# Nine channel blocks by seven products instead of eight, and the seam from up to down

## The chip, the cores and the metric

The kernel runs on one core of a Trainium2 chip. Its time is the device time of one execution in microseconds (us). The core has five engines that run side by side, each through its own list of instructions in order: TensorE (PE, matrix products, with its weight loads as PEld), VectorE (DVE), ScalarE (ACT), GpSimd (POOL) and SyncE (SP, which here issues most of the DMA transfers). An instruction waits until the semaphores that it names have been raised by what it depends on, and everything behind it on its engine waits with it.

## The reference

One layer of a hybrid encoder trunk on 512 tokens of width 1024, in float32. Four token mixers and a gated merge come first, then cross-attention, then the gated MLP that this text is about:

```python
hf = _rms_norm(x, norm_ffn_pre[l])
u = _dwconv_causal(hf @ w_up[l], ffn_dw[l]) + ffn_dw_b[l]
u_g, u_v = jnp.split(u, 2, axis=-1)
yff = (jax.nn.silu(u_g) * u_v) @ w_down[l]
x = x + _rms_norm(yff, norm_ffn_post[l])
```

`w_up` is 1024 x 5632 (2816 gate channels and 2816 value channels), `w_down` 2816 x 1024. The convolution runs along the tokens, has three taps and a weight per channel.

## The kernel before, in words

**Precision.** Each factor of a product is split into a high and a low half (`split_weights`, `split_to`: ACT rounds the high half, called `wh`, `hth`, `tokh`, with a CAST; DVE subtracts for the low half, `wl`, `htl`, `tokl`). `mm3` (line 245 through `matmul`) then makes three matmuls: high by high, high by low, low by high. Split weights lie in four buffers each for high and low, used in turn (`weights_tile`), so a tile can be split when PE has left the tile four before it.

**Up.** The 2816 channels are 22 blocks (NF) of 128, numbered j. A *plain* block (`plain(j, i)`; i is 0 for gate, 1 for value) is 8 x 3 matmuls of 512 tokens into one PSUM bank, so a channel block is 48 of them. A *seven* (`seven(j)`) forms gate and value of one j together: seven half-size products by a Strassen-like scheme, 7 x 4 x 3 = 84 matmuls of 256 tokens. POOL forms three sums of weights for it (lines 1755 to 1759), its weights are split in four tiles (loads a, b, c, d), and five pieces of work follow, `body_a` to `body_d` and `end`, called a to e here. c and e both use the tile that c splits (`z.w`). The seven's two results lie in one bank of `sc` (`z.r1`) and one of `tr` (`z.r2`); pieces are joined by ACT copies (`mu`) and DVE adds (lines 1786, 1797, 1801).

After the matmuls `done` puts the bias and the last tap on with ACT and adds the other two taps with DVE (line 627, called taps here); `product_of` then makes silu(gate) * value into `qa`, one tile of four parts for each pair of channel blocks (11 pairs, q = 0 to 10).

The jobs of up run interleaved: a(j), plain(j-1, 0), b, first half of plain(j-1, 1), c, d, second half, e, for j = 5, 7, ... 19. The blocks 20 and 21 follow as four plain blocks.

**Down.** It multiplies the 11 pairs, again by seven products per pair: M1, M6 (job 0) and M5, M7 (job 1) in a first phase, M2, M3 and M4 in a second. (q, job) names a weight tile of the first phase. Each M has two banks, one for each token tile t. The tiles come by SP (`load_parts`, line 594) into four buffers `dw` in turn, two of which are the `wq` buffers of the sevens; ACT and DVE split them (lines 1673 and 1674), and split the activations of pair q too (`activations`). For this, sums of a pair's four parts are needed (`down_sums`, lines 1684 to 1686, three DVE instructions of 256 columns), into places made free by `down_places`. Line 1920 is a POOL difference for the second phase.

**Order.** `run_blocks` fetches (loads and splits) about four jobs ahead of the one whose matmuls it writes. The order on each engine that results is then made by a scheduler when the program is built.

Of the kernel before, what the change touches and what calls it, by code (L numbers as in the profile page):

```python
# [25 lines left out]
P = 128  # L26
S = 512
# [59 lines left out]
def hybrid_layer(ctx: ExitStack, tc: tile.TileContext, a: dict, out: bass.AP):  # L87
# [520 lines left out]
    def seven_banks(phase):  # L608
        names = (("M2", "sc"), ("M3", "tr"), ("M4", "mm")) if phase else (("M1", "sc"), ("M6", "tr"), ("M5", "mm"),
                                                                         ("M7", "av"))  # L610
        return {name: [bank(tag) for _ in range(2)] for name, tag in names}
# [1027 lines left out]
    def open_ffn():  # L1639
        bg.drain("n1")  # L1640
        close(ns.work_)
        close(ns.xp_)
        close(ns.xm_)
        ns.fp_, ns.fp = new_pool("ffn", False)
        ns.work = ns.fp
        ns.quart = [ns.fp.tile([P, 4, S // 2], F32, tag=f"qa{q}", name="qa") for q in range(NF // 2)]
        ns.tok = [ns.fp.tile([P, 4, 4, S // 2], F32R, tag=n, name=n) for n in ("tokh", "tokl")]
        ns.post = ns.fp.tile([P, D], F32, name="g_ffn")
        ns.dw = {"dw": 1}
        G.dma_start(ns.post, a["norm_ffn_post"][0].partition_broadcast(P))  # L1650
# [25 lines left out]
    def down_places(tag, n):  # L1676
        x = ns.fp.tile([P, 2 * n, S // 2], F32, tag=tag, name="pairs")
        ns.pair_sums += [x[:, 2 * i:2 * i + 2] for i in range(n)]

# [8 lines left out]
    def up_jobs():  # L1688
# [126 lines left out]
        def early_places():  # L1815
            ns.pair_sums = []
            down_places(f"qa{NF // 2 - 1}", 2)

# [7 lines left out]
        pairs = {j: seven(j) for j in range(5, NF - 2, 2)}  # L1826
# [6 lines left out]
        for q, j in enumerate(pairs, EARLY - 1):  # L1833
# [25 lines left out]
            if j == NF - 3:  # L1859
                yield then(lambda: down_places("z7", 2))  # L1860
            yield d
            yield then(lambda j=j, f=second_half: f(j - 1))
            if j == NF - 3:
                yield then(sums_of(2))
# [3 lines left out]
        def late_places():  # L1868
            down_places("tokh", NF // 2 - 4)
            ns.quart[-1] = ns.fp.tile([P, 4, S // 2], F32, tag="tokl", name="qa")  # L1870

        yield then(late_places)
        yield plain(NF - 2, 0, sums_of(3))
        yield plain(NF - 2, 1, sums_of(4))
        yield plain(NF - 1, 0, sums_of(5))
        yield plain(NF - 1, 1)

    def down_jobs():
# [16 lines left out]
        def activations(phase, q):  # L1895
# [16 lines left out]
            else:  # L1912
# [3 lines left out]
                if 6 <= q + 2 < pairs:  # L1916
# [91 lines left out]
        def ends():  # L2008
# [5 lines left out]
            def whole(name, t, x, pieces=1):  # L2014


                for c in range(pieces):
                    cut = slice(c * S // pieces, (c + 1) * S // pieces)
                    ps = bank("av") if c else None
# [30 lines left out]
        def body(phase, q, job, ws):  # L2050
            if (q, job) == (0, 0):
                banks.update(seven_banks(phase))
# [61 lines left out]
```

## Time and profile before

| what | us |
|---|---|
| median of 3 runs (1032.75 to 1033.51) | 1033.33 |
| the profiled execution's own time | 1035.12 |
| its span, first to last instruction | 1033.3 |
| PE / DVE / ACT / POOL busy | 1024.4 / 864.0 / 534.4 / 263.5 |
| granted PE clock, mean over the span | 0.999 |

The profile is one execution. Its page gives the busy time of each engine, a chain of work followed back from the last instruction, and groups of instructions by source line. The trace behind it can be asked for the waits of an engine, for the busy time of each engine in given stretches, and for single instructions in order of time: start, length, engine, line, operation, output<-inputs, partitions x elements, count, and in brackets how long the engine had been idle before and what released it. A matmul's end is modelled; the distance from one start to the next is what a matmul costs in a dense stretch.

### The profile page before, as it was taken

The page shows a single profiled execution, that of the slowest core. Times are in us where ns is not written, and L with a number is a line of the kernel's source. Part 1 is how long each engine was busy: PE and PEld are TensorE (multiplying, and loading weights), DVE is VectorE, ACT ScalarE, POOL GpSimd, SP SyncE. Part 2 cuts the span into 40 slices and gives each one's busy share as a digit, 9 for nine tenths or more (in the row PEclk, how much of TensorE's full clock was granted, in tenths as well). Part 3 has the DMA queues.
Part 4 walks back from the last instruction along what each step waited for, and adds up shares of the span by engine and source line. Part 5 has one row for each costly group of instructions (what it writes and reads, how often), then busy time and mean ns, then how long its engine had stood idle before and what let it go on. Part 6 is the DMA issues. An engine that isn't in the chain of part 4 may idle for free.

```text
span 1033.3 us, 15189 instructions
## 1 busy us (share of the span) xinstructions
PE 1024.4 (99%) x5477; PEld 883.0 (85%) x5477; DVE 864.0 (84%) x1323; ACT 534.4 (52%) x893; POOL 263.5 (26%) x270
## 2 busy tenths in 40 slices
PE   9999999999999999999999999999999999999997
PEld 8888888888888988888888899999899899888886
DVE  7899999796878667888687898787989897799886
ACT  5322222376565466766543665655455455466662
POOL 4001000100011214442100031039177557226202
PEclk9999999999999999999999999999999999999999
DMA  7954344844434255767448834233456576626852
GB/s 248 317 176 106 104 147 143 280 143 115 141 102 140 63 157 137 195 184 188 154 146 264 262 123 123 82 97 116 134 164 209 180 225 210 197 81 187 274 161 82
DMA packets 194128, 169.40 MB, mean 164 GB/s; under 512 B 25295, under 2 KB 165692, under 8 KB 194053
## 3 DMA queue, kind: packets, MB, share of 16 engines
q1 hardware_dynamic: 187315, 145.08, 46.9%
q10 hardware_dynamic: 4178, 14.82, 3.9%
q0 software_dynamic: 2560, 8.54, 2.7%
q8 instruction: 43, 0.70, 0.3%
q14 instruction: 32, 0.26, 0.1%
HBM read 142.18 MB, written 26.23 MB: 163 GB/s over the span
## 4 chain that ended last, share of the span: by engine, by line
PE 95%; DVE 2%; DMA 1%; ACT 1%; issue 1%; POOL 0%; POOLq 0%; DVEq 0%; SPq 0%; ACTq 0%
PE ps_mm L245 41%; PE ps_av L245 26%; PE ps_tr L245 15%; PE ps_sc L245 11%; PE ps_tr L251 1%; PE ps_mm L463 1%; PE ps_av L463 1%; DVE e L860 0%; DMA xs<-in_x 0%; DMA ptl<-turned 0%; DVE e L1133 0%; DVE ptl L879 0%; ACT wh L202 0%; ACT e L1139 0%; DVE qk L820 0%
## 5 line engine op out<-in xcount | busy, mean ns | idle before, releaser
L202 ACT CAST wh<-wr 128x1024 fp32r<-128x1024 f32 (+1 forms) x124 | 129.5, 1046 | 188.6 <-PE ps_mm L245 70.4
L203 DVE TENSOR_TENSOR wl<-wr,wh 128x1024 fp32r<-128x1024 f32 (+1 forms) x124 | 165.3, 1334 | 30.0 <-ACT wh L202 29.5
L245 PE MATMUL ps_mm<-hth,wh 128*128 128x512 f32 (+1 forms) x472 | 173.5, 376 | 0.1
L245 PE MATMUL ps_mm<-htl,wh 128*128 128x512 f32 (+1 forms) x472 | 173.5, 376 | 0.0
L245 PE MATMUL ps_mm<-hth,wl 128*128 128x512 f32 (+1 forms) x472 | 173.2, 375 | 0.0
L245 PEld LDWEIGHTS ps_mm<-hth,wh 128*128 128x128 f32 x472 | 87.1, 188 | 15.7 <-ACT hth L164 0.3
L245 PEld LDWEIGHTS ps_mm<-hth,wl 128*128 128x128 f32 x472 | 87.0, 188 | 15.7
L245 PEld LDWEIGHTS ps_mm<-htl,wh 128*128 128x128 f32 x472 | 87.0, 188 | 15.2
L245 PE MATMUL ps_av<-htl,wh 128*128 128x512 f32 (+1 forms) x264 | 97.8, 370 | 0.0
L245 PE MATMUL ps_av<-hth,wh 128*128 128x512 f32 (+1 forms) x264 | 97.7, 370 | 0.0
L245 PE MATMUL ps_av<-hth,wl 128*128 128x512 f32 (+1 forms) x264 | 97.6, 370 | 0.0
L700 DVE SCALAR_TENSOR_TENSOR y<-y,par,y 128x508 f32<-128x508 f32 (+29 forms) x120 | 83.0, 733 | 0.0
L245 PEld LDWEIGHTS ps_av<-htl,wh 128*128 128x128 f32 x264 | 49.6, 188 | 8.1
L245 PEld LDWEIGHTS ps_av<-hth,wl 128*128 128x128 f32 x264 | 49.7, 188 | 8.0
L245 PEld LDWEIGHTS ps_av<-hth,wh 128*128 128x128 f32 x264 | 49.6, 188 | 8.0
L1673 ACT CAST wh<-dw 128x1024 fp32r<-128x1024 f32 x32 | 33.7, 1052 | 21.6 <-PE ps_av L245 8.1
L1674 DVE TENSOR_TENSOR wl<-dw,wh 128x1024 fp32r<-128x1024 f32 x32 | 39.6, 1243 | 5.5 <-ACT wh L1673 5.5
L245 PE MATMUL ps_tr<-htl,wh 128*128 128x512 f32 (+1 forms) x112 | 40.6, 363 | 0.0
L245 PE MATMUL ps_tr<-hth,wh 128*128 128x512 f32 (+1 forms) x112 | 40.6, 362 | 0.0
L245 PE MATMUL ps_tr<-hth,wl 128*128 128x512 f32 (+1 forms) x112 | 40.5, 361 | 0.0
L1920 POOL TENSOR_TENSOR qa<-qa 128x256 f32<-128x256 f32 x11 | 26.6, 2425 | 49.2 <-DVE wr L1674 25.2
L1127 POOL TENSOR_SCALAR fbias<-ck,cq 128x128 f32<-128x128 f32 (+3 forms) x32 | 21.3, 671 | 67.9 <-DVE st L1133 62.4
(558 smaller groups left out, 2739.1 us busy)
## 6 DMA issues: line engine op xcount, KB each, us to landing
wr<-in_w_in SPq DMA_DIRECT2D x38, 512.0 KB
wr<-in_w_gate SPq DMA_DIRECT2D x32, 512.0 KB
wr<-in_w_up SPq DMA_DIRECT2D x28, 512.0 KB
dw<-sums SPq DMA_DIRECT2D x44, 256.0 KB
wr<-in_w_branch SPq DMA_DIRECT2D x16, 512.0 KB
wq<-in_w_up SPq DMA_DIRECT2D x16, 512.0 KB
wp<-in_w_down ACTq DMA_DIRECT2D x14, 512.0 KB
sums<-wp ACTq DMA_DIRECT2D x14, 512.0 KB
```

The lines of the kernel that those rows point to most:

```text
L202: last_weights[:] = [order(A.copy(hi, raw[:, :n])).ins, low.tensor_tensor(lo, raw[:, :n], hi.bitcast(F32), ALU.subtract).ins]
L203: low.tensor_tensor(lo, raw[:, :n], hi.bitcast(F32), ALU.subtract).ins]
L245: steps_of[:] = [PE.matmul(ps, lhs, rhs, start=start, stop=stop, skip_group_check=again).ins]
L251: turns.append(PE.transpose(ps, x, ident[:n, :n]).ins)
L463: keep(PE.matmul(banks[c][:, :S // 2], w[p == 1][:, k, c * P:(c + 1) * P], ht[p == 2][:, i * 4 + k, :S // 2], start=(i, p, k) == (0, 0, 0) ...
L700: ins = V.scalar_tensor_tensor(dst[:, s:], src[:, :S - s], pc("conv_dw", k * 4 + j), dst[:, s:], ALU.mult, ALU.add)
L1127: G.tensor_scalar(bias[:, :w], ck[j][:, :w], -1.0, cq[:, qt, head:head + 1], ALU.mult, ALU.add)
L1673: A.copy(hi, x)
L1674: return V.tensor_tensor(lo, x, hi.bitcast(F32), ALU.subtract).ins
L1920: G.tensor_tensor(z[:, 1], z[:, 2], z[:, 1], ALU.subtract)
```

## The change

Block 21 becomes a ninth seven, interleaved with the plain block 20 as the others are. It then needs its working tiles (`tokh`, `tokl`, `z7`, the `wq` buffers) to the very end of up. So the places move: the last pair's activations get a tile of their own (`qlast`) where the gain `g_ffn` lay, the gain is loaded into `tokl` when up is over, and the sums of pair 3 are made after the last product of up, those of pairs 4 and 5 during down. Since the last seven holds a bank of `sc` and one of `tr`, M1, M6, M5, M7 are put in `mm`, `av`, `sc`, `tr` instead of `sc`, `tr`, `mm`, `av`, and the second phase likewise.

```diff
-    def seven_banks(phase):
-        names = (("M2", "sc"), ("M3", "tr"), ("M4", "mm")) if phase else (("M1", "sc"), ("M6", "tr"), ("M5", "mm"),
-                                                                         ("M7", "av"))
-        return {name: [bank(tag) for _ in range(2)] for name, tag in names}
+    def seven_banks(phase, tags=("sc", "tr", "mm", "av")):
+        names = ("M2", "M3", "M4") if phase else ("M1", "M6", "M5", "M7")
+        return {name: [bank(tag) for _ in range(2)] for name, tag in zip(names, tags)}
...
-        ns.post = ns.fp.tile([P, D], F32, name="g_ffn")
+        ns.last = ns.fp.tile([P, 4, S // 2], F32, name="qlast")
...
-        G.dma_start(ns.post, a["norm_ffn_post"][0].partition_broadcast(P))
...
+    def load_gain():
+        ns.post = ns.fp.tile([P, D], F32, tag="tokl", name="g_ffn")
+        G.dma_start(ns.post, a["norm_ffn_post"][0].partition_broadcast(P))
...
             down_places(f"qa{NF // 2 - 1}", 2)
+            ns.quart[-1] = ns.last
...
-        pairs = {j: seven(j) for j in range(5, NF - 2, 2)}
+        pairs = {j: seven(j) for j in range(5, NF, 2)}
...
-            if j == NF - 3:
+            if j == NF - 1:
                 yield then(lambda: down_places("z7", 2))
             yield d
             yield then(lambda j=j, f=second_half: f(j - 1))
-            if j == NF - 3:
+            if j == NF - 1:
                 yield then(sums_of(2))
...
         def late_places():
+            sums_of(3)()
             down_places("tokh", NF // 2 - 4)
-            ns.quart[-1] = ns.fp.tile([P, 4, S // 2], F32, tag="tokl", name="qa")
+            load_gain()
 
         yield then(late_places)
-        yield plain(NF - 2, 0, sums_of(3))
-        yield plain(NF - 2, 1, sums_of(4))
-        yield plain(NF - 1, 0, sums_of(5))
-        yield plain(NF - 1, 1)
...
-                if 6 <= q + 2 < pairs:
+                if 4 <= q + 2 < pairs:
                     down_sums(q + 2, low)
...
-                    ps = bank("av") if c else None
+                    ps = bank("tr") if c else None
...
-                banks.update(seven_banks(phase))
+                banks.update(seven_banks(phase, ("mm", "av", "sc", "tr")))
```

The order moves on every engine where up ends. DVE before, from the low half of the weights (0,0,1) to that of (0,1,0), `wl_9002`, whose raw tile is `dw_8907`; `c_8894` is block 20 and `c_8991` block 21:

```order
L1674 TENSOR_TENSOR wl_8963<-dw_8904,wh_8962 128x1024
L627 SCALAR_TENSOR_TENSOR c_8894<-ps_av_8920,par0_398,c_8894 128x510
L1686 TENSOR_TENSOR qa_6904<-pairs_8800,qa_6904 128x256
L627 SCALAR_TENSOR_TENSOR c_8894<-ps_av_8920,par0_398,c_8894 128x511
L1684 TENSOR_TENSOR pairs_8861<-qa_6905 128x256
L1685 TENSOR_TENSOR pairs_8861<-qa_6905 128x256
L1706 TENSOR_TENSOR qa_8862<-c_8894 128x512
L1674 TENSOR_TENSOR wl_9002<-dw_8907,wh_9001 128x1024
```

All of this stood beside the matmuls of the plain blocks of 20 and 21.

DVE in the changed program, from the add behind c of the last seven (`ps_tr0_8869`, line 1799) on: the split of (0,0,1) (`wl_9002` now), a tap of block 20, the add behind d (`ps_sc_8868`), a tap,

```order
L1799 TENSOR_TENSOR ps_tr0_8869<-ps_tr0_8869,mu_8870 128x256
L1672 TENSOR_TENSOR wl_9002<-dw_8963,wh_9001 128x1024
L626 SCALAR_TENSOR_TENSOR c_8926<-ps_av_8979,par0_398,c_8926 128x510
L1803 TENSOR_TENSOR ps_sc_8868<-ps_sc_8868,mu_8870 128x256
L626 SCALAR_TENSOR_TENSOR c_8926<-ps_av_8979,par0_398,c_8926 128x511
```

and then, up to the split of (0,1,0) (`wl_9023` from `dw_8966`; `wl_9098` is (0,1,1)):

```order
L1686 TENSOR_TENSOR pairs_9018<-qa_6903 128x256
L1687 TENSOR_TENSOR pairs_9018<-qa_6903 128x256
L1672 TENSOR_TENSOR wl_9098<-dw_8992,wh_9097 128x1024
L1708 TENSOR_TENSOR qlast_6914<-c_8926 128x512
L1672 TENSOR_TENSOR hth_8995<-qa_6902,hth_8995 128x512
L1688 TENSOR_TENSOR qa_6903<-pairs_9018,qa_6903 128x256
L1672 TENSOR_TENSOR hth_8995<-pairs_7191,hth_8995 128x512
L626 SCALAR_TENSOR_TENSOR c_9039<-ps_sc_8868,par0_398,c_9039 128x510
L1672 TENSOR_TENSOR hth_8995<-pairs_9018,hth_8995 128x512
L1686 TENSOR_TENSOR pairs_9083<-qa_6905 128x256
L1687 TENSOR_TENSOR pairs_9083<-qa_6905 128x256
L1672 TENSOR_TENSOR wl_9023<-dw_8966,wh_9022 128x1024
```

The split of (0,1,0) has moved behind the adds of the seven, behind the sums of pairs 2 and 3 and behind splits of activations. After it come a tap, a 512-wide split, a tap and the split of (0,2,0) (`wl_9125`).

PE in the changed program. The last rows of up are e's, into `ps_tr0_8869` with c's tile `wh_8897`; nine matmuls with the tiles of pair 0 follow, and then, with `wh_9097` and `wl_9098` of (0,1,1) and `wh_9022` and `wl_9023` of (0,1,0):

```order
L245 MATMUL ps_sc_9105<-wh_9097,hth_8995 128x512
L245 MATMUL ps_tr1_9107<-wh_9097,hth_8995 128x512
L245 MATMUL ps_sc_9105<-wl_9098,hth_8995 128x512
L245 MATMUL ps_tr1_9107<-wl_9098,hth_8995 128x512
L245 MATMUL ps_mm_9101<-wh_9022,hth_8995 128x512
L245 MATMUL ps_mm_9102<-wh_9022,hth_8995 128x512
L245 MATMUL ps_av_9103<-wh_9022,hth_8995 128x512
L245 MATMUL ps_av_9104<-wh_9022,hth_8995 128x512
L245 MATMUL ps_sc_9105<-wh_9097,hth_8995 128x512
L245 MATMUL ps_tr1_9107<-wh_9097,hth_8995 128x512
L245 MATMUL ps_mm_9101<-wl_9023,hth_8995 128x512
```

So the low half of (0,1,0) is read by the twentieth matmul after e. In the buffers `wh_9022` is the fourth tile after `wh_8897`. The matmul that first reads (0,2,1), `wh_9151`, is 32 matmuls after this last row, and the first that reads the activations of pair 3, `htl_8996`, four after that one.

ACT in the changed program, from the cast of (0,2,0) (`wh_9124`) on; `wh_9170` is (0,3,0), `wh_9216` (0,4,0), `wh_9151` (0,2,1), `wh_9197` (0,3,1), and `qa_6904` belongs to pair 3:

```order
L1671 CAST wh_9124<-dw_9019 128x1024
L1671 CAST htl_8996<-pairs_9083 128x512
L1706 ACTIVATE c_9039<-c_9039 128x512
L1671 CAST wh_9170<-dw_9121 128x1024
L1671 CAST htl_8996<-qa_6905 128x512
L1671 CAST wh_9216<-dw_9167 128x1024
L1671 CAST htl_8996<-pairs_9018 128x512
L1671 CAST wh_9151<-dw_9086 128x1024
L1671 CAST wh_9197<-dw_9140 128x1024
L1671 CAST hth_8995<-qa_6907 128x512
L1671 CAST htl_8996<-qa_6904 128x512
```

The casts of (0,3,0) and (0,4,0) stand ahead of that of (0,2,1) here. The raw tiles `dw_9121` and `dw_9167` lie in the buffers of (0,1,0) and (0,2,0).

## The prediction, on record before the changed kernel ran

> **What bounds the kernel now.** I read the page first, then the waits of TensorE (PE), then the stretches around the place that is changed.
>
> ```profile
> span 1033.3 us, 15189 instructions
> PE   1024.4 (99%) x5477; PEld 883.0 (85%) x5477; DVE 864.0 (84%) x1323; ACT 534.4 (52%) x893; POOL 263.5 (26%) x270
> ...
> PE 95%; DVE 2%; DMA 1%; ACT 1%; issue 1%; POOL 0%; POOLq 0%; DVEq 0%; SPq 0%; ACTq 0%
> ```
>
> PE works for 1024.4 of 1033.3 us and carries 95% of the chain of waits. Its list of waits over the whole run has three entries:
>
> ```profile
> PE ps_mm L404 <- DVE e L354: 1.3, 1, 1.3
> PE ps_av L245 <- DVE ptl L879: 0.4, 1, 0.4
> PE ps_tr L447 <- DVE nt L442: 0.2, 1, 0.2
> ```
>
> None lies in the feed-forward part. So a matmul less there is time won, and any new wait of PE is time lost. The stretches (columns: length, then busy time of PE, PEld, DVE, ACT, POOL, clock, DMA) show what is scarce where up ends (921.2) and down begins:
>
> ```profile
> 901.00:912.00 11.00, 11.00 (x52) 9.15 (x51) 11.00 (x17) 7.66 (x10) 1.36 (x1) 1.00 0.31 89
> 912.00:921.20 9.20, 9.20 (x42) 7.62 (x41) 9.05 (x17) 2.41 (x5) 0.30 (x1) 1.00 0.36 119
> 921.20:932.00 10.80, 10.80 (x48) 8.83 (x47) 9.73 (x15) 9.16 (x15) 5.66 (x4) 1.00 0.18 52
> 932.00:943.00 11.00, 11.00 (x50) 9.07 (x49) 10.77 (x14) 7.12 (x9) 11.00 (x3) 1.00 0.69 218
> ```
>
> VectorE (DVE) is full there as well (40.6 of 42 us), and PE does not wait only because DVE's results come early. How early they come after the change is the question.
>
> **What PE saves.** From the chain (start, length): the same product of a seven starts at 752.65 and, six rounds later, at 877.37; and the last plain blocks follow each other at full rate.
>
> ```profile
> 752.65 2.83 PE ps_tr L245 x24
> ...
> 877.37 2.83 PE ps_tr L245 x24
> ...
> 910.49 5.44 PE ps_mm L245 x24
> 915.93 5.44 PE ps_av L245 x24
> ```
>
> One round is one channel block by seven products and one plain: (877.37 - 752.65) / 6 = 20.79 us. Two plain channel blocks are four times 5.44 = 21.76 us. The change makes the last such pair a round: **-0.97 us** on PE. A 512-wide matmul costs 5.44 / 24 = 0.227, twenty-four 256-wide ones 2.83. Down has the same matmuls as before, and only their banks are renamed.
>
> **What comes in the way.** The four buffers of split weights go round, so a tile is split once PE has left the tile four before it. The tile to watch is the first weight of down's second pair, (0,1,0). Before:
>
> ```profile
> 915.74 1.06 ACT L1673 CAST wh<-dw 128x1024 fp32r<-128x1024 f32 x1 [2.66 <-PE ps_mm L245]
> 917.00 1.22 DVE L1674 TENSOR_TENSOR wl<-dw,wh 128x1024 fp32r<-128x1024 f32 x1
> 926.33 0.39 PE L245 MATMUL ps_sc<-wl,hth 128*128 128x512 f32 x1
> ```
>
> Its buffer was that of plain block (21,0); PE left it at 915.7, the low half was ready at 918.2 and used at 926.3, 8.1 us later. In the changed order the tile four before it is c's, and c's weights are kept for the seven's last product e, the last matmuls of up. PE wants the new tile's low half 19 matmuls after e, 19 x 0.227 = 4.3 us. The steps from one DVE instruction to the next:
>
> ```profile
> 908.02 1.21 DVE L1674 TENSOR_TENSOR wl<-dw,wh 128x1024 fp32r<-128x1024 f32 x1
> 909.15 0.74 DVE L627 SCALAR_TENSOR_TENSOR c<-ps_mm,par,c 128x510 f32<-128x510 f32 x1
> 909.81 0.68 DVE L1674 TENSOR_TENSOR wr<-qa,wr 128x512 fp32r<-128x512 f32 x1
> 910.41 0.69 DVE L1674 TENSOR_TENSOR wr<-pairs,wr 128x512 fp32r<-128x512 f32 x1
> ...
> 912.27 0.42 DVE L1684 TENSOR_TENSOR pairs<-qa 128x256 f32<-128x256 f32 x1
> 912.61 0.42 DVE L1685 TENSOR_TENSOR pairs<-qa 128x256 f32<-128x256 f32 x1
> ```
>
> A 1024-wide split takes 1.13, a tap 0.66, a 512-wide instruction 0.60, a 256-wide one 0.34. I count from the end of product c, where DVE must stand still for PE (in the round before it did so for 2.00 us):
>
> ```profile
> 895.98 0.43 DVE L1797 TENSOR_TENSOR ps_tr<-ps_tr,mu 128x256 f32<-128x256 f32 x1 [2.00 <-PE ps_tr L245]
> ```
>
> - DVE to the end of (0,1,0): 2 splits 2.26, 3 taps 1.98, 4 of 512 2.40, 7 of 256 2.38, and the split itself 1.22: **10.24**.
> - PE to the matmul that reads it: 29 of 512 (6.57; 1 of plain (20,1) and 9 of down's first pair beside d and e, 19 behind e) and d and e (2.83), less 0.16, since c's last matmul ends 0.28 after its start and the next starts after 0.12: **9.24**.
>
> ```profile
> 869.83 0.28 PE L245 MATMUL ps_sc<-tokl,wh 128*128 128x256 f32 x1
> 869.95 0.28 PE L245 MATMUL ps_sc<-tokh,wl 128*128 128x256 f32 x1
> ```
>
> **First wait: 1.0 us.** What is late next? The four buffers of raw weights go round too: the load of (0,3,0) waits for this split and that of (0,4,0) for the split of (0,2,0). From split to use such a load takes, before:
>
> ```profile
> 931.36 1.22 DVE L1674 TENSOR_TENSOR wl<-dw,wh 128x1024 fp32r<-128x1024 f32 x1
> ...
> 932.61 0.33 SPq L594 DMA_DIRECT2D dw<-in_w_down  x1
> ...
> 936.67 1.06 ACT L1673 CAST wh<-dw 128x1024 fp32r<-128x1024 f32 x1 [1.02 <-DMA dw<-sums]
> ```
>
> 936.67 - 932.58 = 4.1 us. Split (0,2,0) ends at 10.15 + 0.66 + 0.60 + 0.66 + 1.22 = 13.3, so (0,4,0) can be cast at 17.4. On ScalarE (ACT) that cast stands ahead of the one of (0,2,1). ACT's steps:
>
> ```profile
> 921.18 1.05 ACT L1673 CAST wh<-dw 128x1024 fp32r<-128x1024 f32 x1 [3.71 <-PE ps_av L245]
> 922.14 0.61 ACT L1673 CAST htl<-qa 128x512 fp32r<-128x512 f32 x1
> 922.66 0.62 ACT L1673 CAST htl<-pairs 128x512 fp32r<-128x512 f32 x1
> ```
>
> 0.96 for a 1024 cast, 0.52 for a 512 one: (0,2,1) starts at 17.4 + 0.96 + 0.52 = 18.9 and is there at 19.9. PE, let go at 10.24, comes to it 32 matmuls (7.25) later, at 17.5: **second wait 2.4 us**. Four matmuls on (20.8) PE wants the cast of pair 3's activations, which ACT ends at 18.9 + 0.96 + 0.96 + 0.52 + 0.62 = 21.9: **third wait 1.1 us**. Behind that, PE's order and ACT's run in step again, a pair of tiles to a pair of tiles, and I count no more. The sum: -0.97 + 1.0 + 2.4 + 1.1 = **+3.5 us**.
>
> Bounds of the waits. If every load were instant, ACT would still hold (0,4,0) until PE leaves (0,2,0), 26 matmuls after 10.24: 16.3, and the second wait is still 1.3: +2.4 in all. From above, DVE beside GpSimd (POOL):
>
> ```profile
> 910.64 1.66 POOL L1920 TENSOR_TENSOR qa<-qa 128x256 f32<-128x256 f32 x1 [25.21 <-DVE wr L1674]
> ...
> 924.17 1.12 POOL L1920 TENSOR_TENSOR qa<-qa 128x256 f32<-128x256 f32 x1 [11.87 <-DVE htl L1674]
> ...
> 924.62 1.23 DVE L1674 TENSOR_TENSOR hth<-qa,hth 128x512 fp32r<-128x512 f32 x1
> ```
>
> A 0.68 split took 1.23 beside one L1920. One such before the first wait and one before the second make +1.1: +4.6. But beside the L1920 of 910.64 the two 512-wide rows from 910.41 on kept their 0.60, and the rows that I price with are of the very kinds that stand in the list; so I keep +3.5.
>
> Edits at nothing:
>
> - The four operand sums of the last seven go to POOL, which had been idle for 25.21 us at 910.64. In the round before the last of them stood here:
>
> ```profile
> 875.17 1.29 POOL L1759 TENSOR_TENSOR s<-wq,sums 128x512 f32<-128x512 f32 x1
> ...
> 884.47 2.04 DVE L203 TENSOR_TENSOR wl<-wq,wh 128x1024 fp32r<-128x1024 f32 x1
> ...
> 989.63 1.29 DVE L1986 TENSOR_TENSOR o<-o,g_ffn 128x512 f32<-128x512 f32 x2
> ```
>
>   A round later it ends near 897, and c near 895.9 + 20.8 = 916.7. Uncovered, the four would cost d's wait, a few us.
> - The gain's load stands on POOL behind e, near 921, and is wanted at 989.6. Behind it wait only L1920 rows, whose results the second phase of down reads. Nothing is lost unless it took over 60 us.
> - The old order on SP let down's first loads start long before; now that of (0,0,1) waits for c's split, whose row of the round before is the one at 884.47: it ends near 884.5 + 2.0 + 20.8 = 907.3, and 4.1 us later, at 911.4, the load is there, 5 us before c ends.
> - The taps that free the banks for the second tiles of M5 and M7 end at 10.15 + 0.66 + 0.60 + 0.74 = 12.2 and at 13.2 + 0.34 + 0.60 + 0.68 + 0.74 = 15.6; PE comes there 12 and 26 matmuls after 10.24, at 13.0 and 16.1. They are covered by 0.8 and 0.5, and by as much as DVE is later they are waits of their own.
> - The sums of pairs 4 and 5 are counted where they stand in DVE's list; ahead of the second wait they are already in the steps.
>
> **Rivals.**
> 1. *The cover holds* (not slower): DVE gets to (0,1,0) 1.0 us sooner and the loads need no more than 4.1 - 2.4 = 1.7 us, ACT's line too being shorter. For it: DVE had 2.00 us of standing still in the round before. Against: that stop is in front of c's add, where my count begins. Then 1033.3 - 1.0 = 1032.4.
> 2. *Only the first wait*: loads issued together land sooner, and the delay itself gives ACT time. 1033.3 - 0.97 + 1.0 = 1033.4. Against: ACT's order holds even with instant loads.
> 3. *POOL slows DVE throughout*: five 1024-wide splits at the 2.04 of the row at 884.47 instead of 1.22 add up to 4 us, half of it before a wait: 1036.8 + 2 = 1038.8. Against: POOL's sums of the last seven end some 20 us before c does, and then it has only one short L1920 per pair.
>
> 4. *The clock drops in a wait.* At the end of the run, without matmuls:
>
> ```profile
> 1027.00:1030.00 3.00, 0.00 (x0) 0.00 (x0) 2.29 (x4) 0.51 (x2) 1.22 (x2) 1.00 0.45 175
> 1030.00:1033.00 3.00, 0.00 (x0) 0.00 (x0) 0.54 (x2) 0.00 (x0) 0.00 (x0) 0.66 0.48 175
> ```
>
> The clock stays at 1.00 for 3 us of idleness and is 0.66 in the next three. No wait of mine is 3 us long; if two run together, three microseconds at 0.66 cost 1.0: 1037.8. [...]
>
> **How the numbers follow.** The profiled execution took 1035.12 us for its span of 1033.3; the runs' median is 1033.33. The difference is worked out within the span and put on the median: 1033.33 + 3.5 = **1036.8**. Chances: the forecast 0.64 (own range 1035.6 to 1038.2), rival 1 0.12, rival 2 0.10, rival 3 0.09, rival 4 0.05. The range 1033.2 to 1038.6 leaves out rival 1 and most of rival 3. Within 0.2% (2.1 us, about what can be told from no change here) end rivals 1 and 2: 0.21 with the tails; faster by more needs twice what PE saves: 0.02; slower 0.77.
>
> **What would show it.** In the profile after: rounds of 20.8 us to the end of up; in PE's waits a new one on DVE's `wl` split of L1672 of about 1 us, then two on ACT casts of L1671 of about 2.4 and 1.1, all within 14 us of the end of up; SP issuing the load of (0,4,0) some 3 us after PE resumed. Wrong would be a list of waits as short as today's, or waits on taps (L626), which would mean that the banks decide.

## The result, and the profile after

The changed kernel takes **1038.87 us** (median of 4 runs, 1037.50 to 1039.21), the kernel before on the same chip 1033.39 (4 runs): 5.5 us more, a ratio of 1.0052 with a 95% interval of 1.0034 to 1.0069. The forecast was 1036.8 with a range up to 1038.6: the direction was right, the size 2 us too small, and the result lies 0.3 us outside the range.

The page of the profiled execution after (its own time 1038.73), span and busy times, and the chain of waits by engine:

```profile
span 1036.9 us, 15275 instructions
PE 1023.0 (99%) x5513; PEld 883.9 (85%) x5513; DVE 863.9 (83%) x1328; ACT 537.0 (52%) x898; POOL 267.2 (26%) x274
...
PE 93%; DVE 3%; DMA 2%; issue 1%; ACT 1%; POOL 0%; POOLq 0%; DVEq 0%; SPq 0%; ACTq 0%
```

PE is busy 1.4 us less than before, and the span is 3.6 us longer. PE's list of waits after, over the whole run (total, times, longest):

```profile
PE ps_sc L245 <- ACT wh L1671: 1.8, 1, 1.8
PE ps_mm L404 <- DVE e L354: 1.3, 1, 1.3
PE ps_tr L447 <- DVE nt L442: 1.3, 1, 1.3
PE ps_tr L251 <- DVE nt L300: 1.3, 1, 1.3
PE ps_mm L245 <- DVE wl L1672: 0.8, 1, 0.8
PE ps_av L245 <- ACT pth L877: 0.4, 1, 0.4
```

Two waits are the forecast ones: 0.8 on DVE's `wl` and 1.8 on ACT's `wh`. The third is not in the list. L251 is new too, and the prediction says nothing of it: it stands at 697 us, where the feed-forward part opens, 200 us ahead of the changed round. (L447 lies near 500 us, where both kernels have the same order on every engine; it is 0.2 to 1.7 in the traces of this study, whatever the kernel.)

The place itself in the timeline of PE and ACT after:

```profile
927.15 0.50 PE L245 MATMUL ps_mm<-wl,hth 128*128 128x512 f32 x1 [0.83 <-DVE wl L1672]
...
936.62 1.12 PE L245 MATMUL ps_sc<-wh,hth 128*128 128x512 f32 x2 [1.81 <-ACT wh L1671]
937.54 1.05 PE L245 MATMUL ps_tr<-wh,hth 128*128 128x512 f32 x2
938.61 0.79 PE L245 MATMUL ps_mm<-wh,htl 128*128 128x512 f32 x1
...
934.05 1.05 ACT L1671 CAST wh<-dw 128x1024 fp32r<-128x1024 f32 x1 [1.59 <-DMA dw<-sums]
935.01 0.61 ACT L1671 CAST htl<-pairs 128x512 fp32r<-128x512 f32 x1
935.53 1.99 ACT L1671 CAST wh<-dw 128x1024 fp32r<-128x1024 f32 x2
```

It is the picture that was forecast: ACT waits 1.59 for a late load, casts that tile first, and only then the tile (0,2,1) that PE stands still for. From start to start PE loses 1.0 in the first wait and 1.97 in the second. But the matmuls behind the second wait are slow: pairs take 0.92 and 1.07 instead of 0.45. The stretches, cut at 3.41 us (length, busy time of PE, PEld, DVE, ACT, POOL, then the granted clock):

```profile
929.95:933.36 3.41, 3.41 (x16) 2.76 (x16) 3.41 (x9) 1.57 (x2) 0.00 (x0) 1.00 0.53 160
933.36:936.77 3.41, 1.60 (x8) 0.99 (x7) 3.41 (x6) 2.72 (x4) 1.77 (x1) 1.00 0.40 123
936.77:940.18 3.41, 3.39 (x8) 2.19 (x9) 3.41 (x6) 2.41 (x4) 3.41 (x1) 0.50 0.57 171
940.18:943.60 3.42, 3.42 (x17) 2.82 (x16) 3.42 (x7) 0.55 (x1) 3.42 (x1) 1.00 0.76 230
```

For exactly one such stretch the granted clock is 0.50. Eight matmuls from 936.62 on take 3.73 us instead of 1.81: 1.92 us more, and under it the third wait disappears, because ACT catches up while PE is slow. So here -0.97 + 1.0 + 1.97 + 1.92 = +3.9 us.

And the opening of the feed-forward part, before and then after:

```profile
696.38 1.29 DVE L300 SCALAR_TENSOR_TENSOR nt<-res,st_r,g_pre 128x1024 f32<-128x1024 f32 x1 [0.91 <-POOL st_r L290]
...
696.48 0.59 POOL L1650 DMA_DIRECT2D g_ffn<-in_norm_ffn_post  x1
697.09 9.88 POOL L1663 TENSOR_TENSOR qa<-hth,htl 128x1024 f32<-128x1024 f32 x4
```

```profile
695.04 3.41 DVE L300 SCALAR_TENSOR_TENSOR nt<-res,st_r,g_pre 128x1024 f32<-128x1024 f32 x1 [0.92 <-POOL st_r L290]
...
694.98 10.44 POOL L1661 TENSOR_TENSOR qa<-hth,htl 128x1024 f32<-128x1024 f32 x4
```

Before, POOL issued the gain's load first and began the token sums 0.7 us after DVE had begun `nt`. With the load moved away, POOL begins its sums 0.06 us ahead of `nt` (694.98 and 695.04), `nt` takes 3.41 us instead of 1.29, and PE waits 1.3 us for it. In later and moved (below) the first sum begins 0.07 us ahead of `nt`, which takes 3.41 again; in dead and best it begins 0.71 and 4.31 us behind the start of `nt`, which takes 1.28. Why `nt` is longer beside a sum the traces do not show.

To see where each kernel wins or loses, I subtract, for the same matmul, its start in the trace of before from its start in another trace, at 690, 712 and 897 us of before (ahead of the changed round the order on PE is the same) and at PE's last matmul. What each stretch adds, in us, for the kernels of this study:

| kernel | to 690 | 690 to 712 | 712 to 897 | 897 to PE's last |
|---|---|---|---|---|
| changed | -1.25 | +1.05 | -0.24 | +3.98 |
| changed, again | -1.55 | +1.09 | -0.24 | +4.47 |
| banks | +4.48 | 0.00 | -0.24 | 0.00 |
| sums | -1.03 | +0.07 | -0.24 | +0.03 |
| fill | +0.86 | +1.23 | -0.24 | +3.41 |
| later | +0.08 | +1.01 | -0.08 | +0.57 |
| dead | -1.30 | +0.08 | -0.07 | +6.04 |
| moved | +0.53 | +12.77 | +2.48 | 0.00 |
| best | +1.41 | +0.07 | -0.08 | -0.80 |
| five | -0.68 | +1.23 | -0.19 | +0.78 |
| pool | -0.69 | +1.23 | +0.02 | +1.98 |
| both | -2.29 | +0.07 | -0.24 | +1.03 |
| eight | -2.27 | +0.07 | -0.24 | -1.09 |

But for banks, the first column is scatter from one execution to the next in work that the edits leave alone. The trace of before has it on the slow side: its execution took 1035.12, and the four medians of the kernel before in the experiments below are 1033.1 to 1034.0. That is why the two spans lie only 3.6 apart while the medians lie 5.5 apart. The change itself costs the second and the last column: 1.05 + 3.98 = 5.0 in one trace, 1.09 + 4.47 = 5.6 in the other. The medians lie 5.5 and 5.8 apart (intervals 3.5 to 7.1 and 4.3 to 7.0), which agrees.

### The profile page after: what moved, and what is told of

The parts are those of the page before. It is cut to its first block, busy times and chain, and to the rows that moved or that the text cites. A ratio compares the mean times of both kernels' runs of the same rounds, so it can differ in the third digit from the quotient of the medians.

```text
span 1036.9 us, 15275 instructions
## 1 busy us (share of the span) xinstructions
PE 1023.0 (99%) x5513; PEld 883.9 (85%) x5513; DVE 863.9 (83%) x1328; ACT 537.0 (52%) x898; POOL 267.2 (26%) x274
## 4 chain that ended last, share of the span: by engine, by line
PE 93%; DVE 3%; DMA 2%; issue 1%; ACT 1%; POOL 0%; POOLq 0%; DVEq 0%; SPq 0%; ACTq 0%
PE ps_mm L245 40%; PE ps_av L245 26%; PE ps_tr L245 14%; PE ps_sc L245 10%; PE ps_tr L251 1%; DMA ptl<-turned 1%; PE ps_mm L463 1%; PE ps_av L463 1%; DMA turned<-e 0%; DVE wl L1672 0%; DMA xs<-in_x 0%; DMA wr<-in_w_up 0%; DVE nt L300 0%; DVE c L626 0%; DMA dw<-sums 0%
## 5 line engine op out<-in xcount | busy, mean ns | idle before, releaser
L202 ACT CAST wh<-wr 128x1024 fp32r<-128x1024 f32 (+1 forms) x122 | 127.4, 1048 | 188.3 <-PE ps_mm L245 66.8
L203 DVE TENSOR_TENSOR wl<-wr,wh 128x1024 fp32r<-128x1024 f32 (+1 forms) x122 | 161.0, 1321 | 28.3 <-ACT wh L202 26.9
L245 PE MATMUL ps_mm<-hth,wh 128*128 128x512 f32 (+1 forms) x464 | 170.3, 375 | 0.0
L245 PE MATMUL ps_mm<-htl,wh 128*128 128x512 f32 (+1 forms) x464 | 170.3, 375 | 0.0
L245 PE MATMUL ps_mm<-hth,wl 128*128 128x512 f32 (+1 forms) x464 | 170.0, 375 | 0.0
L245 PE MATMUL ps_av<-htl,wh 128*128 128x512 f32 (+1 forms) x256 | 94.6, 370 | 0.0
L245 PE MATMUL ps_av<-hth,wh 128*128 128x512 f32 (+1 forms) x256 | 94.5, 369 | 0.0
L245 PE MATMUL ps_av<-hth,wl 128*128 128x512 f32 (+1 forms) x256 | 94.5, 369 | 0.0
L878 DVE TENSOR_TENSOR ptl<-ptl,pth 128x384 fp32r<-128x384 f32 (+3 forms) x42 | 20.5, 510 | 15.3 <-ACT pth L877 15.3
```

What stands on the lines that cost most here:

```text
L202: last_weights[:] = [order(A.copy(hi, raw[:, :n])).ins, low.tensor_tensor(lo, raw[:, :n], hi.bitcast(F32), ALU.subtract).ins]
L203: low.tensor_tensor(lo, raw[:, :n], hi.bitcast(F32), ALU.subtract).ins]
L245: steps_of[:] = [PE.matmul(ps, lhs, rhs, start=start, stop=stop, skip_group_check=again).ins]
L878: V.tensor_tensor(lo, raw, hi.bitcast(F32), ALU.subtract)
```

## The experiments

### The change once more (again)

No edit.

> The changed kernel once more, unedited, to see how well the difference repeats and where it lies. The profile of it puts the time so: -0.97 us for the round, 1.0 for the first wait (PE on DVE's wl), 1.97 for the second (PE on ACT's wh), 1.92 for eight matmuls at a granted clock of 0.54 behind the second wait. Together +3.9 us. Theory A (all of the difference lies at the end of up and the first four pairs of down): again about +3.9 in the spans, and the 5.5 between the medians holds something that the profile of before had by chance; then the median is 4 to 5 us above before. Theory B (the change costs something else as well, ahead of that place or behind it): again 5.5 in the times, and the rows ahead of 900 us or behind 945 us lie apart by 1.5 us or more.

1039.27 us against 1033.50: ratio 1.0055 (1.0042 to 1.0068). The difference repeats, so theory A falls and B holds: there is a second place, 200 us ahead of the round. The waits at the end of up in this trace were 0.8, 1.6 and 0.8 on ACT's `htl`: here the third wait of the forecast shows.

### The banks alone (banks)

```diff
-        names = (("M2", "sc"), ("M3", "tr"), ("M4", "mm")) if phase else (("M1", "sc"), ("M6", "tr"), ("M5", "mm"),
-                                                                         ("M7", "av"))
+        names = (("M2", "mm"), ("M3", "av"), ("M4", "sc")) if phase else (("M1", "mm"), ("M6", "av"), ("M5", "sc"),
+                                                                         ("M7", "tr"))
...
-                    ps = bank("av") if c else None
+                    ps = bank("tr") if c else None
```

> The kernel before with the banks alone: M1, M6, M5, M7 in mm, av, sc, tr and the second phase likewise. Theory A (the banks decide nothing; the new waits come from buffers and from DVE's and ACT's order): within 0.5 us of before, no new wait of PE over 0.5 us. Rival (the new waits are waits for banks): 1 us or more slower, with a wait of PE near the end of up.

1037.21 against 1033.50: 1.0031 (1.0018 to 1.0044). By the time the rival seems to win, by the trace it does not. From 897 us on the same matmuls stand where they stood, to 0.00 us. The loss lies ahead of 640 us: with this edit the scheduler also put cross-attention in another order, PE waits there, and the clock falls behind that wait:

```profile
PE ps_mm L245 <- DVE htl L165: 1.6, 1, 1.6
```

```profile
624.87:628.28 3.41, 1.56 (x11) 1.36 (x12) 3.41 (x6) 2.02 (x5) 1.55 (x5) 1.00 0.77 225
628.28:631.69 3.41, 3.41 (x18) 3.41 (x18) 3.41 (x4) 1.88 (x2) 0.00 (x0) 0.51 0.36 109
```

The changed kernel does not have that other order in cross-attention. So the banks cost nothing where they are used; the kernel's time would have told a wrong story.

### The sums of pairs 4 and 5 alone (sums)

```diff
-        yield plain(NF - 2, 1, sums_of(4))
-        yield plain(NF - 1, 0, sums_of(5))
+        yield plain(NF - 2, 1)
+        yield plain(NF - 1, 0)
...
-                if 6 <= q + 2 < pairs:
+                if 4 <= q + 2 < pairs:
```

> The kernel before with the sums of pairs 4 and 5 inside down alone (in the place where they stand after the change). They are 6 DVE instructions of 0.34 us, 2.0 us of DVE moved into stretches where DVE is busy all the time. Theory A (DVE has its results early enough in the old order): within 0.5 us of before. Rival (DVE is the bound of the first pairs of down, and what is moved into them is paid): 1 to 2 us slower, with waits of PE on DVE between 925 and 950 us.

1034.42 against 1033.50: 1.0007 (0.9998 to 1.0015), and +0.03 us from 897 us on. In the old order DVE is early enough: alone, this part of the change is free.

### PE kept at work in the second wait (fill)

```diff
+        ns.zero = ns.fp.tile([P, P], F32R, name="zero")
+        V.tensor_tensor(ns.zero, ident, ident, ALU.subtract)
...
+            if (phase, q, job) == (0, 2, 1):
+                full = parts[0, 2][0][:, :2].rearrange("p a b -> p (a b)")
+                for _ in range(8):
+                    matmul(banks["M6"][1], ns.zero, full, False, False, True)
```

> The changed kernel with eight more matmuls of 128x512 with a stationary tile of zeros, which add nothing to the bank of M6, in the place where PE would stand still in the second wait. They take 8 x 0.227 = 1.8 us, so that this wait of 1.8 us shrinks to 0.8 or less; nothing else is taken away. Theory A (the standing still lowers the clock): the granted clock stays at 1.00 in the 4 us behind it, and the matmuls there take 0.227 us again; the third wait that I forecast, hidden by the slow matmuls, comes out with 0.6 to 1.1 us, so the time falls by 0.3 to 1.2 us against the changed kernel. Rival B (the clock falls for another reason, such as all engines and the DMA at work at once): the matmuls behind take about 0.46 us again at a clock near 0.5, and the time is that of the changed kernel or up to 1 us longer.

1038.35 against 1033.50 (1.0045, 1.0033 to 1.0057); the changed kernel had 1039.27 beside it, so 0.9 us less, which the two intervals cannot tell apart. The waits left are 0.8, 0.6 and 0.3, and the clock stays up in the stretches behind:

```profile
PE ps_mm L245 <- DVE wl L1674: 0.8, 1, 0.8
PE ps_sc L245 <- ACT wh L1673: 0.6, 1, 0.6
...
PE ps_mm L245 <- ACT htl L1673: 0.3, 1, 0.3
```

```profile
935.60:939.00 3.40, 3.34 (x15) 2.42 (x13) 3.40 (x6) 2.52 (x4) 1.71 (x1) 1.00 0.39 114
939.00:942.40 3.40, 2.56 (x10) 1.82 (x11) 3.40 (x6) 2.54 (x4) 3.40 (x1) 1.00 0.63 184
```

Theory A holds: with DVE busy for all of both stretches, ACT for 2.52 and 2.54 and PE at work for 3.34 and 2.56 us, the clock does not fall, and all five runs have a mean clock of 0.998 or 0.999 where seven of nine of the changed kernel have 0.996 or 0.997. The gain is small, since 1.8 us of empty matmuls take the place of 1.8 us of waiting; only the slow matmuls are saved, less the third wait that they had hidden.

### The sums one pair later (later)

```diff
-                if 4 <= q + 2 < pairs:
-                    down_sums(q + 2, low)
+                if 4 <= q + 1 < pairs:
+                    down_sums(q + 1, low)
```

> The changed kernel, but inside down the sums of a pair are made one pair later (behind the splits of pair q those of q + 1, not q + 2). Theory A (the long waits at the end of up come from what stands ahead of the splits in DVE's and ACT's order, not from the round itself): worked through with the rows' durations, the first wait shrinks to 0.5 us, the second and third become one of 1.0 us, no wait is long enough to lower the clock; -0.97 + 1.5 = +0.5 us there. With 1.3 us that the changed kernel loses where the feed-forward part opens (below, dead and moved) that is 1.8 us over before, some 3.5 us less than the changed kernel. Rival B (the buffers of c and of (0,0,1) and the late loads set the waits whatever DVE does): the waits stay at 0.8 and 1.8 us, and the time stays 5.5 us over before.

1035.75 against 1033.96: 1.0018 (1.0009 to 1.0027), 1.8 us over before as foretold. From 897 us on the loss is 0.57 where 0.5 was expected; the opening keeps its 1.01.

```profile
PE ps_tr L251 <- DVE nt L300: 1.2, 1, 1.2
PE ps_mm L245 <- ACT htl L1671: 0.8, 1, 0.8
...
PE ps_mm L245 <- DVE wl L1672: 0.2, 1, 0.2
```

Two digits of the code, and 3.4 us of the 4.0 at the end of up are gone, with the buffers as they were. So the sums, free in the old order, have a place in the new one that is enough to make most of the price: DVE has no room left there (in the changed kernel it is busy for all of 929.95 to 943.60), each 0.34 us in front of a split delays it, with it the next load, and with that ACT. (The scheduler makes a new order of the whole place for each such edit, so this is the effect of the edit with its order.)

### The gain's load: back in its old place (dead), and moved alone (moved)

Dead, an edit of the changed kernel:

```diff
         ns.last = ns.fp.tile([P, 4, S // 2], F32, name="qlast")
+        G.dma_start(ns.last.rearrange("p a b -> p (a b)"), a["norm_ffn_post"][0].partition_broadcast(P))
```

> The changed kernel with a load of the gain put back in its old place on POOL, ahead of the token sums (into qlast, where nothing needs it; the gain is still loaded into tokl at the end). In the profile of the changed kernel the token sums (POOL, L1661, 1024 wide, four in 10.4 us) start at 694.98, 2.1 us sooner than before, and the DVE instruction beside them (nt, L300) takes 3.41 us instead of 1.29; PE waits 1.3 us for it. Theory C (the issue of this load had held POOL back until DVE was done; moving it away costs 1.3 us): nt takes 1.3 us again, the wait of PE for nt (L251) is gone, and the time falls by 1.3 us against the changed kernel, to 4.2 us over before. Rival D (that wait comes from something else, or is made up for behind it): the time stays 5.5 us over before.

Moved, an edit of the kernel before:

```diff
-        G.dma_start(ns.post, a["norm_ffn_post"][0].partition_broadcast(P))
+    def load_gain():
+        G.dma_start(ns.post, a["norm_ffn_post"][0].partition_broadcast(P))
...
             ns.quart[-1] = ns.fp.tile([P, 4, S // 2], F32, tag="tokl", name="qa")
+            load_gain()
```

> The kernel before with the gain's load alone moved, from the opening of the feed-forward part to the end of up; on PE, DVE, ACT and SP every instruction stands where it stood, and on POOL the issue of this load now stands behind the first two token sums. Theory C: nt (L300) at about 696 us takes about 3.4 us instead of 1.3, PE waits 1.3 us for it, and the kernel is 1.3 us slower than before. Rival D: within 0.4 us of before.

Dead took 1039.07 against 1033.96: 1.0045 (1.0030 to 1.0060). That interval holds both expectations; its trace had two stretches at half clock at the end of up (+6.04) instead of one, so its time says nothing of the opening. The trace does: `nt` takes 1.28 again, the wait on L251 is gone, and 690 to 712 costs 0.08 instead of 1.05.

```profile
694.97 1.28 DVE L300 SCALAR_TENSOR_TENSOR nt<-res,st_r,g_pre 128x1024 f32<-128x1024 f32 x1 [0.92 <-POOL st_r L290]
...
695.07 0.59 POOL L1648 DMA_DIRECT2D qlast<-in_norm_ffn_post  x1
695.68 9.89 POOL L1662 TENSOR_TENSOR qa<-hth,htl 128x1024 f32<-128x1024 f32 x4
```

Moved took **1048.88** against 1033.96: 1.014 (1.0125 to 1.0155), 15 us slower by the place of one load on POOL. Its rows, first the waits of PE, then DVE and POOL:

```profile
PE ps_mm L245 <- DVE c L627: 11.6, 1, 11.6
...
PE ps_tr L251 <- DVE nt L300: 1.0, 1, 1.0
```

```profile
696.63 3.41 DVE L300 SCALAR_TENSOR_TENSOR nt<-res,st_r,g_pre 128x1024 f32<-128x1024 f32 x1 [0.92 <-POOL st_r L290]
...
706.72 13.87 DVE L203 TENSOR_TENSOR wl<-wr,wh 128x1024 fp32r<-128x1024 f32 x1 [3.96 <-ACT wh L202]
...
707.57 1.29 POOL L1757 TENSOR_TENSOR sums<-wq 128x512 f32<-128x512 f32 x1
708.82 2.39 POOL L1667 TENSOR_TENSOR qa<-qa 128x1024 f32<-128x1024 f32 x1
...
717.18 5.62 POOL L1667 TENSOR_TENSOR qa<-qa 128x1024 f32<-128x1024 f32 x2
```

The part foretold is there: `nt` 3.41, PE's wait 1.0. Theory C holds, D falls. What came on top was not foretold: a split that took 3.01 in the trace of before stands for 13.87 us, while POOL's instructions run one behind another: the token sum in which the split starts and seven more. The first two of these take 1.29 and 2.39, where the trace of before has 2.27 and 3.40. Only the eighth is longer (of the two in the last row above the second, at 719.58, takes 3.21). The same split before, and these two of POOL:

```profile
705.05 3.01 DVE L203 TENSOR_TENSOR wl<-wr,wh 128x1024 fp32r<-128x1024 f32 x1 [4.09 <-ACT wh L202]
...
706.95 2.27 POOL L1755 TENSOR_TENSOR sums<-wq 128x512 f32<-128x512 f32 x1
709.17 3.40 POOL L1665 TENSOR_TENSOR qa<-qa 128x1024 f32<-128x1024 f32 x1
```

The taps queue behind that split and PE waits 11.6 us for them. Behind the first stretch without matmuls the granted clock is 0.50 for 13.65 us; PE stands still for the first 7.7 of these and works at half clock for 5.96:

```profile
713.58:716.99 3.41, 0.00 (x0) 0.00 (x0) 3.41 (x1) 0.00 (x0) 3.41 (x3) 1.00 0.00 0
716.99:730.64 13.65, 5.96 (x14) 4.74 (x15) 13.31 (x12) 5.71 (x7) 5.72 (x3) 0.50 0.30 89
```

### All causes away (best, both, eight) and the buffers alone (five)

The buffers, an edit of the changed kernel: `tokl` becomes four tiles, of which two serve as a fifth pair.

```diff
-        ns.tok = [ns.fp.tile([P, 4, 4, S // 2], F32R, tag=n, name=n) for n in ("tokh", "tokl")]
+        ns.tok = ns.fp.tile([P, 4, 4, S // 2], F32R, tag="tokh", name="tokh")
+        ns.lows = [ns.fp.tile([P, 4, S // 2], F32R, tag=f"tokl{i}", name="tokl") for i in range(4)]
...
+            elif n % 5 == 2 % 5 and n >= 2:
+                hi, lo = (ns.fp.tile([P, D], F32R, tag=f"tokl{i}", name=k) for i, k in enumerate(("wh", "wl")))
```

Five is this alone:

> The changed kernel with tokl in four tiles, two of which are a fifth pair of buffers for the split weights from (0,1,0) on; the sums of the pairs stay where the change put them. Theory A' (either cure is enough: the buffers are what makes ACT and DVE late, the sums stand in front of what is late): worked through with the rows' durations, one wait of 1.3 us on an ACT cast is left, no drop of the clock, -0.97 + 1.3 = +0.4 us at the end of up, and with the 1.05 us of the opening 1.4 us over before. Rival (DVE's load alone makes the waits, as the run with the later sums would allow): waits of 0.8 and 1.8 us and the drop of the clock stay, 5 us over before.

1035.36 against 1033.18: 1.0024 (1.0014 to 1.0034), 2.2 us over before where 1.4 was expected; 0.78 from 897 us on (0.4 expected), one wait of 1.3 on ACT, no drop of the clock, and 1.23 at the opening. Either cure, the buffers or the later sums, takes away more than 3 us of the 3.98, which fits a chain: the buffers set how many tiles can be split ahead of c's add, what is left queues on DVE behind it, and the late split makes the load late. The traces show the middle of it: in the changed kernel the cast of (0,1,0) ends at 923.0 and its split starts only at 925.88, with DVE at work without a break since 916.88. In five DVE makes one more split ahead of c's add and stands still there for 0.70 us instead of 1.84. That the buffers bring this about through the order that the scheduler makes is how I read it.

Best has the buffers, the later sums, and token sums that wait for the last tokens:

```diff
+        x = [h.bitcast(F32)[:, 7, S - 1:S] for h in ns.hf]
+        for i in (0, 3):
+            G.tensor_tensor(raw[i][:, 0, :1], *x, ALU.add)
```

> All causes taken away at once from the changed kernel: the sums one pair later; tokl in four tiles, two of which serve as a fifth pair of buffers for split weights from (0,1,0) on, so that it need not wait for c's; and the token sums made to wait for the last tokens (two POOL instructions one element wide read them first). Theory (these are all the costs of the change): no wait of PE over 0.4 us behind 690 us, nt takes 1.3 us, no drop of the clock, and what is left is the round's -0.97: 1 us faster than before, 1032.5. Rival (the round has a cost of its own that I have not seen, such as more DVE work per round or the clock): not faster than before, 1033.5 or more.

In the trace all is as the theory says: 0.07 at the opening, -0.80 from 897 us on, no wait of PE behind 690 us. But the time is 1034.15 against 1033.96: 1.0002 (0.9993 to 1.0010). Both has the dead load instead of the two small POOL instructions:

> The changed kernel with the fifth pair of buffers, the sums one pair later and the dead load of the gain in its old place on POOL (as in the run of that load alone), so that the opening of the feed-forward part is as in the kernel before. Theory: nothing is lost at the opening, -0.8 us at the end of up (as the trace of the kernel with all causes taken away shows), so 0.8 us faster than before. Rival (POOL's or DVE's later work gives it back): within 0.3 us of before or slower.

1033.97 against 1033.18: 1.0005 (0.9997 to 1.0014). Again not faster, and here the trace shows where it was lost. Up to 981 us of best both traces run in step on PE; then, in down's second phase:

```profile
PE ps_sc L245 <- DVE n L1674: 0.8, 1, 0.8
PE ps_sc L245 <- ACT n L1673: 0.4, 1, 0.4
```

```profile
998.95 1.14 ACT L1673 CAST n<-dw 128x512 fp32r<-128x512 f32 x2 [1.52 <-DMA dw<-sums]
1000.92 1.05 ACT L1673 CAST wh<-dw 128x1024 fp32r<-128x1024 f32 x1 [0.83 <-DMA dw<-in_w_down]
```

Loads that come just in time for a PE that is later are late for one that is earlier. Eight adds a buffer for them:

```diff
-                k = (len(raws) - 2 * pairs) % 7
+                k = (len(raws) - 2 * pairs) % 8
+                if phase and k == 3:
+                    raw = ns.fp.tile([P, D], F32, tag="tokl3", name="dw")
...
-            load(n + (3 if n < 2 * pairs - 2 else 6))
+            load(n + (3 if n < 2 * pairs - 2 else 7))
```

> The kernel of the run before (fifth pair of buffers, sums one pair later, the gain's dead load in its old place) with an eighth buffer for raw weights in down's second phase (tokl's last quarter) and loads issued seven tiles ahead instead of six. In the trace of the run before, PE waits 0.35 and 0.79 us near 1009 us for tiles n of the second phase, behind ACT casts that waited for a load at 998.95 and 1000.92; in the kernel with all causes taken away no such wait is in the trace, though ACT waits for the same loads. Theory E (the 0.8 us won at the end of up is lost again, in some executions, to loads of the second phase that were just in time before): without these waits the kernel is 0.8 us faster than before. Rival F (the 0.8 us is lost elsewhere): again within 0.5 us of before or slower, with no wait of PE in the second phase.

**1032.34** against 1033.07: the medians lie 0.73 us apart, the trace has -1.09 from 897 us on and no wait of PE in down. The ratio is 0.9993 (0.9984 to 1.0002), so by these runs it is not told from no change; the size is near the 0.97 that the round is worth on PE. That the loads took the gain in best and both fits E; shown it is in one trace, and best's own trace had no such wait.

### One long wait (pool)

```diff
+        E = G if q in (3,) else V
         with tc.issue_after(anchor):
-            V.tensor_tensor(t[:, 0], x[:, 1], x[:, 3], ALU.add)
+            E.tensor_tensor(t[:, 0], x[:, 1], x[:, 3], ALU.add)
```

(and the two lines behind it)

> The changed kernel with the three sums of pair 3 on POOL instead of DVE. The planner then puts the work so that, by the rows' durations, the waits run together into one of 3.0 us in the first place. In the traces so far the granted clock changes on a grid of 3.41 us: it was 0.5 for one such window behind a wait of 1.8 us (twice), for two (once), and for four behind a wait of 11.6 us; waits of 0.8 us and 1.3 us had none. Theory (a window of the grid that is idle for more than about half lowers the next one): 3.0 us fill one window by half or more nearly always, so there is a drop behind it, which costs 1.7 us more: -0.97 + 3.0 + 1.7 = +3.7 at the end of up, and with the opening 4.8 us over before. Rival (only a wait over 3.4 us, a whole window, lowers the clock, and the drops seen had another cause): no drop, 3.1 us over before.

1037.21 against 1033.18: 1.0039 (1.0024 to 1.0054), between the two. The profiled execution had the one wait and no drop, and of its four runs only one shows a lower mean clock (0.996):

```profile
PE ps_mm L245 <- DVE wl L1672: 2.7, 1, 2.7
```

```profile
924.98:928.39 3.41, 2.33 (x11) 1.58 (x9) 3.41 (x8) 2.24 (x4) 3.41 (x2) 1.00 0.70 255
928.39:931.80 3.41, 1.78 (x8) 1.47 (x9) 3.41 (x7) 0.62 (x1) 2.66 (x2) 1.00 0.22 63
931.80:935.22 3.42, 3.42 (x17) 2.76 (x16) 3.42 (x7) 2.39 (x4) 1.50 (x1) 1.00 0.69 217
```

A wait of 2.7 us, longer than the one behind which the changed kernel slowed down, and the clock stays: the wait lies in two of the stretches of 3.41 us, and in the one with less work PE was still busy for 1.78. So "nearly always" was wrong, and the rival's bound of a whole idle window is wrong too (the changed kernel had 1.60 us of work in the window, and 0.50 behind it); what held is the order of the two: 0.50 behind 1.60 us of work, 1.00 behind 1.78. From 897 us on the loss is 1.98: -0.97 and the one wait, 2.9 from start to start, make 1.9, with no drop.

## Why the prediction came out as it did

- **The round on PE, -0.97: right.** Where the waits are taken away the end of up gains 0.80 (best) and 1.09 (eight), each in one trace; in the times the gain was not told from nothing.
- **First wait, 1.0: right.** 0.83 of idleness, 1.0 from start to start; DVE took 10.2 us from c's add to the end of the split, as counted.
- **Second wait, 2.4: right in kind and nearly in size.** 1.97, on the cast that was named, behind the cast and the late load that were named. PE came 0.27 us later than counted and the cast was there 0.16 sooner.
- **Third wait, 1.1: right where it shows.** 0.8 in the trace of again; in the profile after it is covered by slow matmuls.
- **The clock, "No wait of mine is 3 us long": wrong.** Rival 4 named the clock, with a bound that was wrong: 3 us, read from the end of the run, where 3 us without matmuls had passed at 1.00. The 0.66 that it reads behind them is a mean of two clocks: in that trace the clock is 1.00 up to 1030.94 and 0.50 from there, behind one whole stretch of 3.41 us (1027.53 to 1030.94) without matmuls. Inside the run the clock was 0.50 behind a wait of 1.8 us. Of the nine runs of the changed kernel with a clock listed, two have 0.998 and took 1037.5 and 1038.2; the others have 0.996 or 0.997 and took 1038.7 to 1040.4. The last column is 3.98 and 4.47 with one slow stretch, where the forecast had 3.5: the clock, net of the third wait that it hides and of the smaller second one, is 0.5 to 1.0 us of the miss.
- **"The gain's load … Nothing is lost": wrong, and it is the step that failed.** I priced the load where it goes and not the hole that it leaves. Its issue had stood in front of POOL's token sums; without it they meet DVE's `nt`. It costs 1.05 to 1.09 us, the other half of the miss: dead takes it away (0.08), moved brings it into the kernel before (`nt` 3.41, a wait of 1.0). Rival 3, POOL against DVE, was right in kind and named the wrong place.
- **Banks at nothing: right**, 0.00 us where they are used, and PE waits for no tap after. **The last seven's operand sums and down's first loads at nothing: right**, PE waits for neither. **The sums of pairs 4 and 5, counted where they stand: right as counted**, but I did not ask what another place for them would do; later shows 3.4 us.
- **The base.** The difference was made within one trace and put on the median. That was sound, and yet the spans of the two profiled executions alone, 3.6 us apart, would have confirmed the forecast by chance: the trace of before was a slow one in work that the change does not touch.

3.5 as forecast, 1.05 for the opening and 0.5 to 1.0 for the clock make 5.0 to 5.5; measured were 5.5 and 5.8.

## What to carry to other kernels

When an instruction moves, price the place that it leaves as well as the place where it goes: what stood behind it on its engine now starts earlier and meets something. A kernel whose bounding engine has no waits has no slack to show either, so an edit that is free in one order (these sums) can be most of the price in another; test it in the order in which it will run. And before a time is believed, line the traces up by the same instructions: the bank edit was 3.7 us slower for a reason 300 us away from the banks.

## What the runs showed of the hardware

**The granted clock was at half in whole stretches of 3.41 us.** It was at 0.50 for one of them in the changed kernel (936.77 to 940.18, behind a wait of 1.8 us), in again (937.77 to 941.18, a wait of 1.6) and in banks (628.28 to 631.69, cut 0.05 us off; a wait of 1.6), for two in dead (936.84 to 943.67, 1.8) and for four in moved (716.99 to 730.64, 11.6). Behind the last matmuls of the changed kernel it falls once more, at 1032.34, which is 28 times 3.41 us behind 936.77. In these traces the clock of a stretch goes with how long PE was busy in the one before. From 1.00, 1.60 us of 3.41 in the changed kernel, 1.6 in banks (1.56 in the row shown under banks), 1.38 in again and 0.00 in moved were followed by 0.50. With 1.78 (pool) and 2.56 (fill) it stayed at 1.00, and so it did in this stretch of again, with L251's wait in it:

```profile
695.43:698.84 3.41, 2.09 (x19) 1.92 (x18) 2.77 (x1) 0.00 (x0) 3.41 (x2) 1.00 0.78 234
698.84:702.26 3.42, 3.42 (x33) 3.42 (x31) 1.29 (x2) 1.07 (x2) 3.42 (x2) 1.00 0.02 5
```

No sharp limit is in these numbers (the ends of matmuls are modelled, which may be why): the stretch in which the matmuls of the run end had 1.59 in pool and 1.63 in sums, and the next one still shows 1.00. And more work than that did not always bring the clock back. In dead the stretch of 933.43 had 1.59, the next ran at 0.50 with this much work, and the one behind it was at 0.50 again:

```profile
936.84:940.25 3.41, 2.62 (x7) 2.02 (x7) 3.41 (x6) 1.49 (x3) 3.41 (x1) 0.50 0.56 167
```

In moved 2.54 at 0.50 was followed by 0.50 too; 3.08 (again) and 3.39 (changed) were followed by 1.00.

So a wait of 1.8 us was followed by a stretch at 0.50, and one of 2.7 us was not: its idle time lies in two stretches, with 2.33 and 1.78 us of work in them. What a stretch at 0.50 costs when it is full of matmuls is 1.7 us by an estimate (half of its 3.41); the eight matmuls of the changed kernel lost 1.92. Nor was it the same from run to run: the nine listed runs of the changed kernel have mean clocks from 0.996 to 0.998.

**A DVE instruction took 13.87 us beside POOL.** It is a 1024-wide split that took 3.01 at the same place in the trace of before, and it lasted over the rest of one POOL instruction and seven whole ones. These seven took 2.33 to 2.40 us (1024 wide) and 1.25 to 1.29 (512 wide); in best the shortest rows of these kinds at this place took 2.40 and 1.29. The times are what the traces show; by what rule one engine came before the other they do not show. Between the two kernels the place of one load, 0.59 us on POOL, is what was edited.
